# Attention and recurrence on TensorE in one written order instead of the scheduler's

## Chip, cores, metric

The kernel runs on one core of one Trainium2 chip. The metric is the device time of one execution in microseconds (us); less is better. TensorE multiplies and transposes, VectorE (DVE), ScalarE (ACT) and GpSimd (POOL) do the elementwise work, SyncE (SP) issues the DMAs.

## The reference

One decoder layer over 2048 tokens of 1024 channels, float32. `h = RMSNorm(x)` is projected once, and four groups of mixers read slices of the projection:

```python
# A, 4 heads of 64: stick-breaking attention, strictly causal
z = q @ k.T * scale;  between = reverse cumsum of log_sigmoid(-z), own term taken off
attn = where(strict, exp(log_sigmoid(z) + between), 0);  out = attn @ v
# B: chunked causal gating (128x128 mixing)
# C, 4 heads of 64: RWKV-7, over time t
sa = -state @ kk_t
state = state * d_t + sa (kk_t a_t)^T + v_t k_t^T;  y_t = state @ r_t
# D, 4 heads of 64: softmax attention with a cumulative log-forget bias, causal
probs = softmax(logits + cum_q - cum_k);  out = probs @ v
x = x + concat(A, B, C, D) @ W_out
x = x + HierMoE(RMSNorm(x));  return RMSNorm(x)
```

## The kernel before

The program has four stages in a row: `in_proj` (the projection), then attention (A and D) together with the recurrence (C), then `out_proj` (the product with W_out, the norm and the router), then the experts. The change is in the second stage, which in the profile lies between some 585 and 1528 us.

**Attention.** `attention` (a generator) walks over 8 heads, first the 4 stick-breaking heads (`sb`), then the 4 softmax heads. A head has 8 blocks `b` of 256 queries (two tiles of 128), and a block has `b // 2 + 1` chunks of up to 512 keys. This document calls the work for one block and one chunk a *step*; there are 20 for a head and 160 in all. A step consists of three pieces on TensorE:

- the *front*: logits of the two query tiles against the chunk, `logits`, lines 375 and 376 (keys are split in a high and a low part), with the mask added on the diagonal by line 378. Behind it, for a stick-breaking head, ScalarE takes a tanh (390), GpSimd an affine map (391) and VectorE a scan from the chunk's end backwards (393, `S`); for a softmax head VectorE adds the key bias and keeps the running maximum (402), and when a tile's last chunk is there, `softmax` forms the bias (408, 409), ScalarE the exponentials with their sums (413), VectorE the reciprocal (415, 416).
- the *transposes* of `S` (line 425), up to 4 per pair of key tiles, into a PSUM bank, which ScalarE copies to SBUF (`tq`, 427).
- the *value products* (line 431), which take `tq` and accumulate in the one bank `o`. When a block is complete, `out` adds its two halves and writes to DRAM (445, 456, 457).

In the old text transposes and value products of a pair stand together in `weigh`. Four PSUM banks serve logits and transposes, one `o`, three the recurrence; 12 SBUF tiles hold `S`.

**Recurrence.** `rwkv` computes C in 8 units (4 quarters of the sequence, 2 pairs of heads). A unit has two `group` generators (two chunks of 128 tokens each, the second one starts two rounds later), the `post` of the last unit and the `front` of the next. `interleave` advances all of them by one piece in turn; this document calls that a *round*, a unit has 24. In a group: two transposes and products (777 to 780), 24 score products (770, in three parts), five levels that invert a triangular matrix in small blocks (832 and 834, then 845; 849 and 850 in the last level), 864 and 870, then 877, 883, 892 to 896, and the state update `M` (913 to 917, 920). Between two levels VectorE works alone: 837 and 839 make `xe` and `yv`, which 845 needs; 846 and 847 make `xc`, which the next 832 needs. Unit 0 is written within `in_proj`.

**What sets the order.** In the program's text units 1 to 7 of the recurrence stand in one piece, then 60 steps of attention, then `route_setup` (tables in DRAM), then the other steps. The framework's scheduler sorts the instructions of every engine by its own estimate of when each can run; nothing is pinned.

```python
            for _ in rw:
                pass
            mix = attention(tc, K, left, sT, sV, cumD, mixT)
            for _ in range(60):
                next(mix)
            route_setup(tc, init, table, gtab, xacc)
            for _ in mix:
                pass
```

Of the kernel before, what the change touches and what calls it, by code (L numbers as in the profile page):

```python
# [307 lines left out]
def attention(tc, K, ctx, sT, sV, cumD, mixT):  # L308
# [17 lines left out]
    class Head:  # L326
# [54 lines left out]
        def spans(self, i):  # L381
            n = (i + 1) * 128
            return [(c, c * 512, min(512, n - c * 512)) for c in range(i // 4 + 1)]

        def sticks(self, i, c, S):
            x0 = c * 512
            w = min(512, (i + 1) * 128 - x0)
            z = self.logits(i, c, w)
# [7 lines left out]
        def softmax(self, i, S, rq):  # L396
            mx = None
            for c, x0, w in self.spans(i):
                z = self.logits(i, c, w)
                S[c] = sp.tile([128, 512], F32, name="S", tag="S")  # L400
                m = tp.tile([128, 1], F32, name="m")
                nc.vector.tensor_tensor_reduce(S[c][:, :w], z, self.nk[c][:, :w], 0.125,
                                               -3.0e38 if mx is None else mx, op0=OP.add, op1=OP.max, accum_out=m)
                mx = m
                yield
            c1 = cq[:, i, self.h:self.h + 1]
            bias = tp.tile([128, 1], F32, name="bias")
            nc.vector.tensor_add(bias, mx, c1)
            nc.vector.tensor_sub(bias, c1, bias)  # L409
            sm = tp.tile([128, 4], F32, name="sm")  # L410
            n = i // 4 + 1
            for c, x0, w in self.spans(i):
                nc.scalar.activation(S[c][:, :w], S[c][:, :w], AF.Exp, bias=bias, accum_out=sm[:, c:c + 1])  # L413
            if n > 1:
                nc.vector.tensor_reduce(sm[:, 0:1], sm[:, 0:n], AX.X, OP.add)
            nc.vector.reciprocal(rq, sm[:, 0:1])

        def weigh(self, b, p, S, o, first, last):
# [7 lines left out]
            tq = tp.tile([128, 512], F32, name="tq")  # L426
            nc.scalar.activation(tq[:, :w], t[:, :w], AF.Copy)  # L427
            for e in range(2):
# [32 lines left out]
        def block(self, b):  # L461
            S = [{}, {}]
            rq = None if self.sb else tp.tile([128, 2], F32, name="rq")
            o = []

            def weigh(p, first, last):
                if first:
                    o.append(po.tile([128, 256], F32, name="o"))
                self.weigh(b, p, S, o[0], first, last)
                if last:  # L470
                    self.out(b, o[0], rq)

            def front(c):
                if b % 2 == 0 and c == b // 2:
                    self.load(c)
                for a in range(2):
                    S[a][c] = sp.tile([128, 512], F32, name="S", tag="S")
                    self.sticks(2 * b + a, c, S[a])
                    yield

            def back(c):
                for p in range(min(2 * c + 1, b), 2 * c - 1, -1):
                    weigh(p, p == b, p == 0)
                    yield

            def front0():
                if b % 2 == 0:
                    self.load(b // 2)
                yield from self.softmax(2 * b, S[0], rq[:, 0:1])

            def mid():
                yield from self.softmax(2 * b + 1, S[1], rq[:, 1:2])

            def back0():
                for p in range(b + 1):
                    weigh(p, p == 0, p == b)
                    yield

            if self.sb:
                return [([front(c)], [], back(c)) for c in range(b // 2, -1, -1)]  # L500
            return [([front0()], [mid()], back0())]

    prev = iter(())
    for sb in (True, False):
        for h in range(NH):
            H = Head(h, sb)
            for b in range(8):
                for first, second, back in H.block(b):
                    for g in first:
                        yield from g  # L510
                    for g in second:
                        for _ in prev:
                            yield
                            next(prev, None)
                            next(g, None)
                        yield from g
                    yield from prev
                    prev = back
    yield from prev


CK = 128
# [83 lines left out]
def rwkv(tc, K, R, ctx, sT, prm, mixT):  # L606
# [358 lines left out]
    def interleave(*gens):  # L965
        gens = list(gens)
        while gens:
            for g in list(gens):
                try:
                    next(g)  # L970
                except StopIteration:
                    gens.remove(g)

    units = [(q, c) for q in range(4) for c in range(2)]
    sh, cur, last = [], [], None
    interleave(front(0, 0, sh, cur))
# [5 lines left out]
    for n, (q, c) in enumerate(units):  # L982
# [10 lines left out]
        interleave(*jobs)  # L993
        if n == 0:
            yield
        last, cur = (q, c, y, bon, sg), nxt
    interleave(post(*last))


# [806 lines left out]
def model(ctx, tc, x, xT, g1, w_in, wsT, bT, mu, w0, w2, a0, a2, g2, k_k, k_a, r_k, gn_w, gn_b, bf, w_out, g2b,  # L1806
# [15 lines left out]
    with tc.tile_pool(name="r_consts", bufs=1) as rp:  # L1822
# [71 lines left out]
```

## Time and profile before

| | us |
|---|---|
| median of 3 runs (lowest, highest) | 2600.77 (2600.74, 2604.18) |
| the profiled execution: its own time | 2600.24 |
| its span, first to last instruction | 2598.5 |
| TensorE busy / VectorE busy in the span | 2444.1 / 1679.6 |
[...]

The span is what the trace shows; 1.74 us lie around it. Busy time of TensorE is the union of its matmuls with modelled ends, so a busy TensorE may still be slowed by its clock or by gaps in its pipeline. A wait is put down to the instruction that came last.

### The profile page before, as it was taken

How to read it: one execution, taken by the hardware profiler on the slowest of the kernel's cores; microseconds unless marked ns; L12 is line 12 of the kernel's file. 1: busy time of each engine (PE TensorE's matmuls, PEld its weight loads, DVE VectorE, ACT ScalarE, POOL GpSimd, SP SyncE). 2: the span in 40 equal slices, each digit the busy share in tenths (PEclk: the TensorE clock that was granted, in tenths of full speed). 3: DMA queues.
4: the chain of work that ended last, by engine and by line, in shares of the span. 5: the costliest groups of instructions: out<-in, count | busy, mean ns of one | idle time of the engine just before them, and what ended most of it. 6: DMA issues, size and time to landing. Idle time of an engine off the chain costs nothing. (4 is left out here: it accounts for less than half of the span.)

```text
span 2598.5 us, 42227 instructions
## 1 busy us (share of the span) xinstructions
PE 2444.1 (94%) x14802; PEld 1753.0 (67%) x14803; DVE 1679.6 (65%) x3881; ACT 1322.4 (51%) x2527; POOL 677.1 (26%) x691
## 2 busy tenths in 40 slices
PE   8999999997989899999999999997999999999994
PEld 6789998874646464656556668874666676676663
DVE  5313402247797879786685756665777787787785
ACT  6201222224665564575566642222666776777774
POOL 2000000016364646331331022222212232222224
PEclk9999999998989998999999999998999999999997
DMA  8510222215121111111101056744979899899995
GB/s 258 163 63 26 80 69 67 71 60 124 35 53 29 47 39 39 47 50 47 49 27 48 10 171 180 234 139 114 339 263 352 309 320 368 292 324 356 328 316 169
DMA packets 241826, 394.73 MB, mean 152 GB/s; under 512 B 65921, under 2 KB 106753, under 8 KB 241608
## 3 DMA queue, kind: packets, MB, share of 16 engines
q1 hardware_dynamic: 222472, 336.68, 39.2%
q0 software_dynamic: 19136, 55.30, 7.6%
q8 instruction: 118, 1.93, 0.3%
q14 instruction: 100, 0.82, 0.1%
HBM read 319.24 MB, written 76.85 MB: 152 GB/s over the span
## 5 line engine op out<-in xcount | busy, mean ns | idle before, releaser
L72 DVE TENSOR_TENSOR wl<-wr,wh 128x1024 fp32r<-128x1024 f32 x366 | 442.4, 1222 | 116.9 <-ACT wh L71 106.8
L71 ACT ACTIVATE wh<-wr 128x1024 fp32r<-128x1024 f32 x366 | 381.4, 1057 | 150.7 <-PE pg L1456 57.9
L393 DVE TENSOR_TENSOR_SCAN S<-S,zero 128x512 f32<-128x512 f32 (+3 forms) x160 | 198.5, 1251 | 48.8 <-POOL S L391 48.6
L152 PE MATMUL p<-hhi,wh 128*128 128x512 f32 x512 | 205.5, 403 | 11.6 <-ACT hhi L112 6.5
L427 ACT ACTIVATE tq<-bk 128x512 f32<-128x512 f32 (+1 forms) x288 | 156.4, 571 | 103.6 <-PE bk L425 83.6
L425 PE MATMUL bk<-ident,S 128*128 128x128 f32 x1088 | 185.1, 291 | 25.0 <-DVE S L393 19.1
L153 PE MATMUL p<-hlo,wh 128*128 128x512 f32 x512 | 205.0, 400 | 0.0
L154 PE MATMUL p<-hhi,wl 128*128 128x512 f32 x512 | 204.5, 400 | 0.0
L431 PE MATMUL o<-tq,v 128*64 128x256 f32 (+1 forms) x1152 | 191.2, 403 | 4.5 <-ACT tq L427 2.6
L425 PEld LDWEIGHTS bk<-ident,S 128*128 128x128 f32 x1088 | 123.2, 144 | 100.7 <-issue 57.6
L156 DVE TENSOR_TENSOR e<-p,rb 128x512 f32<-128x512 f32 x64 | 43.6, 690 | 196.5 <-PE p L154 183.3
L391 POOL TENSOR_SCALAR S<-S 128x512 f32<-128x512 f32 (+3 forms) x160 | 125.6, 794 | 151.7 <-ACT S L390 136.5
L735 POOL TENSOR_TENSOR k<-big,k 128x512 f32<-128x512 f32 x8 | 14.2, 1772 | 550.6 <-DVE big L734 544.6
L375 PE MATMUL bk<-kh,qs 128*128 128x512 f32 (+2 forms) x320 | 148.1, 463 | 5.5 <-POOL qs L351 3.2
L171 PE MATMUL p<-wh,hhi 128*128 128x256 f32 (+1 forms) x512 | 144.5, 282 | 0.0
L172 PE MATMUL p<-wl,hhi 128*128 128x256 f32 (+1 forms) x512 | 144.4, 282 | 0.0
L173 PE MATMUL p<-wh,hlo 128*128 128x256 f32 (+1 forms) x512 | 143.7, 281 | 0.0
L152 PEld LDWEIGHTS p<-hhi,wh 128*128 128x128 f32 x512 | 97.6, 191 | 36.8 <-ACT hhi L112 6.2
L376 PE MATMUL bk<-kl,qs 128*128 128x512 f32 (+2 forms) x320 | 121.4, 381 | 0.0
L413 ACT ACTIVATE S<-S,bias 128x512 f32<-128x512 f32 (+3 forms) x160 | 103.6, 649 | 34.4 <-DVE bias L409 33.9
L71 ACT ACTIVATE wh<-raw 128x512 fp32r<-128x512 f32 (+1 forms) x52 | 27.7, 590 | 178.7 <-PE p L153 171.7
L1453 PE MATMUL pg<-wh,xh 128*128 128x512 f32 x248 | 102.6, 414 | 14.1 <-ACT s L1460 12.6
(559 smaller groups left out, 6153.5 us busy)
## 6 DMA issues: line engine op xcount, KB each, us to landing
wr<-in SPq DMA_DIRECT2D x386, 512.0 KB, 11.1
raw<-in SPq DMA_DIRECT2D x108, 256.0 KB, 4.1
sT<-e SPq DMA_DIRECT2D x64, 256.0 KB, 2.4
raw<-sT SPq DMA_DIRECT2D x128, 128.0 KB, 2.9
mr<-mixT SPq DMA_DIRECT2D x16, 512.0 KB
xt<-in SPq DMA_DIRECT2D x16, 512.0 KB
xacc<-xt SPq DMA_DIRECT2D x16, 512.0 KB, 4.8
h2D<-h SPq DMA_DIRECT2D x16, 512.0 KB, 8.6
```

Source lines behind the costliest of these rows:

```text
L71: nc.scalar.activation(hi, raw, AF.Copy)
L72: nc.vector.tensor_sub(lo, raw, hi.bitcast(F32))
L152: nc.tensor.matmul(p, wh[:, k, ms], hi[j][:, k], start=(k == 0), stop=False)
L153: nc.tensor.matmul(p, wh[:, k, ms], lo[j][:, k], start=False, stop=False)
L154: nc.tensor.matmul(p, wl[:, k, ms], hi[j][:, k], start=False, stop=(k == KD - 1))
L171: nc.tensor.matmul(p, a, wh[:, k], start=first and k == 0, stop=False, skip_group_check=True)
L172: nc.tensor.matmul(p, a, wl[:, k], start=False, stop=False, skip_group_check=True)
L375: nc.tensor.matmul(z[:, :w], q, self.kh[c][:, :w], start=True, stop=False)
L393: nc.vector.tensor_tensor_scan(r, r, K.zero.to_broadcast([128, w]), 1.0 if c == i // 4 else S[c + 1][:, 0:1], op0=OP.mult, op1=OP.add)
L425: nc.tensor.transpose(t[:, x:x + 128], S[a][j // 4][:, (j % 4) * 128:(j % 4) * 128 + 128], K.ident)
L427: nc.scalar.activation(tq[:, :w], t[:, :w], AF.Copy)
L431: nc.tensor.matmul(o[64 * e:64 * e + 64, o0:256], self.v[j // 4][:, j % 4], tq[:, x0:x1], start=first, stop=last, skip_group_check=True)
```

## The change

Units 1 to 7 of the recurrence now yield after every round, attention yields after every step, and both are written in turn under a block in which TensorE keeps the order of the text: 20 steps alone, `route_setup`, then 0.8 of a step per round until the recurrence is through (four rounds out of five are followed by one step, the fifth by none), then the rest. The other engines are still sorted by the scheduler.

Within attention a step is now written as front, value products of an earlier step, transposes of another: transposes come at least two steps (`LAG`) behind their front, value products one step behind their transposes. The two tiles' logits stand together. For a softmax head all chunks of a block get their fronts first, both tiles' bias, sum and reciprocal are made in one instruction each instead of two, and the transposes and products of the block follow one chunk per step. `tq`, `rq` and `m` have four buffers instead of three. The work on TensorE is the same, instruction by instruction.

```diff
-        def weigh(self, b, p, S, o, first, last):
+        def turn(self, b, p, S):
             t = bank()
...
-            tq = tp.tile([128, 512], F32, name="tq")
+            tq = tp.tile([128, 512], F32, name="tq", bufs=4)
             nc.scalar.activation(tq[:, :w], t[:, :w], AF.Copy)
+            return tq
+
+        def weigh(self, b, p, tq, o, first, last):
...
+    LAG = 2
+    ready, turned = [], []
+    n = 0
+
+    def step():
+        if turned:
+            t, weigh = turned.pop(0)
+            weigh(t)
+        if ready and ready[0][0] <= n - LAG:
+            turn, weigh = ready.pop(0)[1]
+            turned.append((turn(), weigh))
...
+                for front, backs in H.block(b):
+                    front()
+                    ready += [(n, f) for f in backs]
+                    step()
+                    n += 1
+                    yield
...
+ALONE = 20
+SHARE = 0.8
...
                 except StopIteration:
                     gens.remove(g)
+            yield
...
-            for _ in rw:
-                pass
             mix = attention(tc, K, left, sT, sV, cumD, mixT)
-            for _ in range(60):
-                next(mix)
-            route_setup(tc, init, table, gtab, xacc)
-            for _ in mix:
-                pass
+            with tc.manual_schedule(engines={mybir.EngineType.PE}):
+                for _ in range(ALONE):
+                    next(mix)
+                route_setup(tc, init, table, gtab, xacc)
+                due = 0.0
+                for _ in rw:
+                    due += SHARE
+                    while due >= 1.0:
+                        next(mix, None)
+                        due -= 1.0
+                for _ in mix:
+                    pass
```

Line numbers of the changed kernel: transposes 420, value products 430, and in the recurrence 11 more than before (832, 834, 845 are 843, 845, 856).

**First place: a stick-breaking head beside the levels of unit 1, on TensorE.** Before (375/376 logits, 425 transposes, 431 value products, 832/834 and 845 the two halves of a level; x4 means four times):

```order
L832 MATMUL bk<-ident,xc 128x128
L834 MATMUL bk<-bd_4722,xc 32x128 x4
L425 MATMUL bk<-ident,S 128x128 x2
L375 MATMUL bk<-kh,qs 128x512
L376 MATMUL bk<-kl,qs 128x512
L375 MATMUL bk<-kh,qs 128x512
L376 MATMUL bk<-kl,qs 128x512
L431 MATMUL o<-tq,v 64x256
L431 MATMUL o<-tq,v 64x128
L845 MATMUL bk<-xe,yv 32x128 x4
L425 MATMUL bk<-ident,S 128x128 x5
L845 MATMUL bk<-xe,yv 32x128 x4
```

The same unit now (420 transposes, 430 value products, 843/845 and 856 the halves of a level), one half of a level of both groups, a whole step, the next half:

```order
L856 MATMUL bk<-xe,yv 32x128 x8
L699 MATMUL bk<-ident,big 128x128 x4
L375 MATMUL bk<-kh,qs 128x512
L376 MATMUL bk<-kl,qs 128x512
L375 MATMUL bk<-kh,qs 128x512
L376 MATMUL bk<-kl,qs 128x512
L430 MATMUL o<-tq,v 64x256
L430 MATMUL o<-tq,v 64x128
L420 MATMUL bk<-ident,S 128x128 x8
L843 MATMUL bk<-ident,xc 128x128
L845 MATMUL bk<-bd_4708,xc 32x128 x4
```

Pieces of two, five and four rows became whole runs; from the first logits product to the last value product of the stage (transposes of `rq`, 455, apart as a kind of their own) runs of one kind number 1141 before and 669 now.

**Second place: a round without a step, in the same unit, now.** 843/845 of both groups and the 856 that needs their results through VectorE stand next to each other:

```order
L420 MATMUL bk<-ident,S 128x128 x8
L843 MATMUL bk<-ident,xc 128x128
L845 MATMUL bk<-bd_4708,xc 32x128 x4
L843 MATMUL bk<-ident,xc 128x128
L845 MATMUL bk<-bd_4722,xc 32x128 x4
L856 MATMUL bk<-xe,yv 32x128 x8
L375 MATMUL bk<-kh,qs 128x512
L376 MATMUL bk<-kl,qs 128x512
```

In the order before, attention lies between the two halves there, as the first fence shows.

**Third place: the end of a unit beside softmax heads.** Before, between the products 892 to 896 and the state update 913 to 917 of unit 5:

```order
L877 MATMUL bk<-kv,akT_4726 128x64 x4
L425 MATMUL bk<-ident,S 128x128 x6
L375 MATMUL bk<-kh,qs 128x256
L376 MATMUL bk<-kl,qs 128x256
L378 LDWEIGHTS identb
L378 MATMUL bk<-fx_mask,identb 128x128
L913 MATMUL bk<-qt,M_7793 64x128 x2
```

Now (888 for 877, 924 for 913):

```order
L888 MATMUL bk<-kv,akT_4726 128x64 x4
L375 MATMUL bk<-kh,qs 128x512
L376 MATMUL bk<-kl,qs 128x512
L375 MATMUL bk<-kh,qs 128x512
L376 MATMUL bk<-kl,qs 128x512
L430 MATMUL o<-tq,v 64x256 x4
L420 MATMUL bk<-ident,S 128x128 x7
L924 MATMUL bk<-qt,M_12786 64x128
```

More of attention now lies at the ends of the units. The table counts fronts (where the logits of one tile stand ahead of a mark and those of the other behind it, half a front). `A` is the stretch until unit 1 begins, `B` runs from the first 777 of a unit to the second group's 849, `C` from there to the next unit:

| stretch | before | now |
|---|---|---|
| A | 13 | 20 |
| B of units 1 to 3 | 55.5 | 36 |
| C of units 1 to 3 | 16.5 | 21 |
| B of units 4 to 7 | 64.5 | 48 |
| C of units 4 to 7 | 10.5 | 31 |
| behind the last unit | 0 | 4 |

## Rows read from the trace of the kernel before

**Rows 1.** The page's head and busy time: engine, us (share), instructions.

```profile
span 2598.5 us, 42227 instructions
PE 2444.1 (94%) x14802; PEld 1753.0 (67%) x14803; DVE 1679.6 (65%) x3881; ACT 1322.4 (51%) x2527; POOL 677.1 (26%) x691
```

**Rows 2.** B of units 1 to 3: busy PE, PEld, DVE, ACT, POOL; clock, DMA share, GB/s.

```profile
678.65:779.30 100.65, 87.68 (x620) 54.02 (x618) 92.13 (x160) 65.58 (x154) 54.60 (x55) 0.93 0.22 54
...
sum 302.35, PE 267.44 PEld 161.79 DVE 276.06 ACT 183.70 POOL 179.72; mean PE 89.14 PEld 53.93 DVE 92.02 ACT 61.23 POOL 59.91
```

**Rows 3.** The same view, C of units 1 to 3 (sum of three).

```profile
sum 105.20, PE 105.20 PEld 71.05 DVE 58.39 ACT 52.17 POOL 37.65; mean PE 35.07 PEld 23.68 DVE 19.46 ACT 17.39 POOL 12.55
```

**Rows 4.** The same view, B of units 4 to 7 (first of four, sum).

```profile
1086.20:1162.70 76.50, 73.08 (x556) 44.79 (x555) 66.50 (x223) 53.20 (x147) 25.06 (x24) 0.98 0.16 42
...
sum 300.30, PE 288.42 PEld 175.74 DVE 257.46 ACT 197.42 POOL 79.11; mean PE 72.10 PEld 43.93 DVE 64.37 ACT 49.36 POOL 19.78
```

**Rows 5.** The same view, C of units 4 to 7 (sum of four).

```profile
sum 125.80, PE 125.80 PEld 85.95 DVE 42.79 ACT 68.05 POOL 22.01; mean PE 31.45 PEld 21.49 DVE 10.70 ACT 17.01 POOL 5.50
```

**Rows 6.** The same view, stretch A and what follows the last unit.

```profile
585.00:678.65 93.65, 79.76 (x592) 50.51 (x592) 64.70 (x116) 44.17 (x105) 50.99 (x54) 0.89 0.41 90
1512.30:1530.00 17.70, 13.78 (x90) 8.13 (x90) 10.00 (x23) 11.81 (x18) 2.38 (x1) 0.92 0.63 213
```

**Rows 7.** Costliest groups, whole span: engine, shapes, count | busy, mean ns | idle before.

```profile
L393 DVE TENSOR_TENSOR_SCAN S<-S,zero 128x512 f32<-128x512 f32 (+3 forms) x160 | 198.5, 1251 | 48.8 <-POOL S L391 48.6
...
L425 PE MATMUL bk<-ident,S 128*128 128x128 f32 x1088 | 185.1, 291 | 25.0 <-DVE S L393 19.1
...
L431 PE MATMUL o<-tq,v 128*64 128x256 f32 (+1 forms) x1152 | 191.2, 403 | 4.5 <-ACT tq L427 2.6
```

**Rows 8.** Groups on VectorE, 580 to 1510 us.

```profile
L402 DVE CUSTOM_DVE_ANT_0 S<-bk,nk,m 128x512 f32<-128x512 f32 (+2 forms) x96 | 61.0, 635 | 25.6 <-PE bk L376 14.2 <-PE bk L378 10.8
...
L408 DVE TENSOR_TENSOR bias<-m,cq 128x1 f32<-128x1 f32 x64 | 18.2, 285 | 0.5
```

**Rows 9.** Timeline of TensorE at full clock: start, us, line, count.

```profile
702.34 0.50 PE L375 MATMUL bk<-kh,qs 128*128 128x512 f32 x1
702.68 0.39 PE L376 MATMUL bk<-kl,qs 128*128 128x512 f32 x1
702.91 0.39 PE L375 MATMUL bk<-kh,qs 128*128 128x512 f32 x1
...
703.37 1.02 PE L937 MATMUL bk<-sg,g 128*128 128x512 f32 x2
```

**Rows 10.** The same at 711.8 and 781.1 us.

```profile
711.78 1.08 PE L431 MATMUL o<-tq,v 128*64 128x256 f32 x8 [0.40 <-DVE oo L445]
712.79 0.38 PE L770 MATMUL bk<-ah,bh 64*128 64x256 f32 x1
...
781.11 1.03 PE L425 MATMUL bk<-ident,S 128*128 128x128 f32 x8
782.08 1.08 PE L431 MATMUL o<-tq,v 128*64 128x256 f32 x8
```

**Rows 11.** Timeline of TensorE in the levels of unit 1, waits in brackets.

```profile
737.63 0.43 PE L845 MATMUL bk<-xe,yv 128*32 128x128 f32 x8 [0.63 <-DVE yv L839]
739.16 0.77 PE L425 MATMUL bk<-ident,S 128*128 128x128 f32 x5 [1.10 <-DVE S L393]
741.14 0.43 PE L845 MATMUL bk<-xe,yv 128*32 128x128 f32 x8 [1.22 <-DVE yv L839]
```

**Rows 12.** Waits of TensorE, 580 to 1510 us: us in total, times, longest.

```profile
PE bk L425 <- DVE S L393: 19.1, 27, 2.6
PE bk L832 <- DVE xc L847: 10.7, 11, 4.7
PE bk L845 <- DVE yv L839: 10.1, 9, 2.7
```

**Rows 13.** Timeline of TensorE, the first product of the next stage.

```profile
1528.34 0.77 PE L1104 MATMUL p<-wh,mh 128*128 128x512 f32 x1 [0.23 <-DVE y L933]
```

More of the change, by code (lines that the diff above doesn't have):

```diff
@@ L379, in logits, with sticks @@
             return z[:, :w]
[L381 to L388, printed above, removed]
+        def sticks(self, i, c, z, S):
+            w = z.shape[-1]
             s = S[c][:, :w]
@@ L462, in block @@
             S = [{}, {}]
-            rq = None if self.sb else tp.tile([128, 2], F32, name="rq")
+            rq = None if self.sb else tp.tile([128, 2], F32, name="rq", bufs=4)
+            mx = [None]
             o = []
[L466 to L471, printed above, removed]
+            top = b // 2
@@ L473, in front @@
+            chunks = range(top, -1, -1) if self.sb else range(top + 1)
+            order = [[p for p in range(min(2 * c + 1, b), 2 * c - 1, -1)] for c in chunks]
+            ends = (order[0][0], order[-1][-1])
             def front(c):
-                if b % 2 == 0 and c == b // 2:
-                    self.load(c)
+                if b % 2 == 0 and c == chunks[0]:
+                    self.load(top)
+                z = []
                 for a in range(2):
+                    i = 2 * b + a
@@ L477, in front @@
                     S[a][c] = sp.tile([128, 512], F32, name="S", tag="S")
[L478 to L503, printed above, removed]
+                    z.append(self.logits(i, c, min(512, (i + 1) * 128 - c * 512)))
+                m = None if self.sb else tp.tile([128, 2], F32, name="m", bufs=4)
+                for a in range(2):
+                    if self.sb:
+                        self.sticks(2 * b + a, c, z[a], S[a])
+                    else:
+                        self.scores(c, z[a], S[a], None if mx[0] is None else mx[0][a], m[:, a:a + 1])
@@ new lines, in front, with turn, weigh @@
+                mx[0] = None if m is None else [m[:, a:a + 1] for a in range(2)]
+                if not self.sb and c == top:
+                    self.softmax(b, S, m, rq)
+            def turn(ps):
+                return [(p, self.turn(b, p, S)) for p in ps]
+            def weigh(t):
+                for p, tq in t:
+                    if p == ends[0]:
+                        o.append(po.tile([128, 256], F32, name="o"))
+                    self.weigh(b, p, tq, o[0], p == ends[0], p == ends[1])
+                    if p == ends[1]:
+                        self.out(b, o[0], rq)
@@ L504, in attention @@
+            backs = [(lambda ps=ps: turn(ps), weigh) for ps in order]
+            for k, c in enumerate(chunks):
+                yield (lambda: front(c)), ([backs[k]] if self.sb else backs if c == top else [])
+    LAG = 2
[8 more added lines that the diff above has]
+            turned.append((turn(), weigh))
     for sb in (True, False):
@@ L507, in attention @@
             for b in range(8):
[L508 to L519, printed above, removed]
+                for front, backs in H.block(b):
[4 more added lines that the diff above has]
+                    yield
+    while ready or turned:
+        step()
+        n += 1
+        yield
+ALONE = 20
+SHARE = 0.8
 CK = 128
@@ L972, in interleave, with run @@
                     gens.remove(g)
+            yield
+    def run(g):
+        for _ in g:
+            pass
     units = [(q, c) for q in range(4) for c in range(2)]
     sh, cur, last = [], [], None
-    interleave(front(0, 0, sh, cur))
+    run(interleave(front(0, 0, sh, cur)))
     yield
@@ L992, in rwkv @@
             jobs.append(front(*units[n + 1], sh, nxt))
-        interleave(*jobs)
         if n == 0:
+            run(interleave(*jobs))
             yield
+        else:
+            yield from interleave(*jobs)
         last, cur = (q, c, y, bon, sg), nxt
-    interleave(post(*last))
+    yield from interleave(post(*last))
 NE = 32
```

38 lines of the change are left out of this document (20 added, 18 removed).

## The prediction

> **What bounds the kernel now.** I read the page first: TensorE is busy 94% of the span, VectorE 65% [rows 1]. That is an average over stages, so I cut the stage of the change, 585 to 1528.34 us [rows 13], by the recurrence, with the view of busy time by stretch. A unit has two faces. In B (scores and levels) of the units that run beside stick-breaking heads, VectorE is busy 276.06 of 302.35 us, 91%, while TensorE has 35 us idle and a granted clock of 0.93 in the first of the three [rows 2]: VectorE sets the pace. In C (the unit's end) TensorE is busy in all of 105.20 us at full clock, VectorE in 58.39 [rows 3]: TensorE sets it. Beside softmax heads TensorE is the bound in both, 288.42 of 300.30 us in B [rows 4] and all of 125.80 us in C [rows 5], with VectorE at 86% in B. So the work that fills one engine alternates with work that fills the other, and a change of order can gain in two ways: by evening this out, and by making TensorE's own stream denser.
>
> The list of TensorE's waits is short: 19.1 us for scans, 10.7 and 10.1 us for the levels of the recurrence [rows 12]. In unit 1 they take 0.6 to 1.2 us each [rows 11].
>
> **The prices.** A step costs TensorE, from start to start at full clock: logits 703.37 - 702.34 = 1.03 us [rows 9], eight value products 712.79 - 711.78 = 1.01 us, eight transposes 782.08 - 781.11 = 0.97 us [rows 10]. A mean step has 1152/160 = 7.2 value products and 1088/160 = 6.8 transposes [rows 7], so 1.03 + 0.91 + 0.82 = 2.76; I take **2.8 us**. On VectorE a stick-breaking step costs two scans of 1.25 = **2.5 us** [rows 7], a softmax step at least two maxima of 0.635 = 1.3 us [rows 8].
>
> **The steps that move.** By the table of fronts in the section on the change:
>
> - A: 7 more steps on a TensorE that has nothing else to take up: 7 x 2.8 = +19.6.
> - B of units 1 to 3: 55.5 - 36 = 19.5 fewer. VectorE loses 19.5 x 2.5 = 48.8 us of 276.06; at its present share of 91.3% that is -53.4. TensorE would then have 267.44 - 54.6 = 213 us of work in 249, so VectorE stays the bound; TensorE's busy share hardly changes (86% for 88%), and I leave the clock as it was.
> - C of units 1 to 3: 4.5 more, TensorE bound: +12.6.
> - B of units 4 to 7: 16.5 fewer, TensorE bound: -46.2. VectorE falls by at least 16.5 x 1.3 = 21 to 236, of 254 us left; the batched bias takes half of line 408's 18.2 us more off it [rows 8]. It comes near to being the bound, so nothing more is credited.
> - C of units 4 to 7: 20.5 more: +57.4.
> - Behind the last unit: 4 more: +11.2.
>
> Together **+1.2 us**. The moves alone are worth nothing: a step that leaves VectorE's stretch saves 2.7 us there and costs 2.8 elsewhere. This is the main reason why I expect little from so large a change.
>
> **Runs of one kind.** The first product of a run takes longer: the first of the logits 702.68 - 702.34 = 0.34 us, the third, of the same shape, 0.23 [rows 9]. I take 0.1 us for a change of kind. The order has 1141 runs before and 669 now, 472 fewer, 47 us if TensorE were the bound everywhere. It is outside B of units 1 to 3, in 943 - 302 = 641 us or 68% of the stage; the runs taken as evenly spread, **-32 us**. Bounds: 0, if the slower start only moves to another place, and -47. I take the middle because the row shows the delay itself.
>
> [...]
>
> **Rounds without a step.** Seven units of 24 rounds, one in five without a step behind it: 34 places where a round stands directly behind the one whose results it needs (second fence of the change: 856 behind 843 and 845). There TensorE must wait for VectorE's `xe` and `yv` or `xc`. B is some 15 rounds long, so 9 of the 34 lie in B of units 1 to 3, where VectorE is the bound anyway and the wait is in its time already. For the other 25 the nearest rows are the waits of the same lines before, 10.1/9 and 10.7/11 or about 1.0 us [rows 12]: **+25 us**. Bounds: 0, since some rounds don't need the one ahead, and 25 x 2.7 = 68 by the longest wait of line 845, when scans stand ahead of `yv` in VectorE's queue. Behind the waiting product the logits of the next step stand, and so all of attention.
>
> **Waits that go.** Transposes come two steps behind their logits, so waits for the scan or the maximum vanish outside the VectorE-bound stretches. TensorE's idle time in B of units 4 to 7 is 300.30 - 288.42 = 11.9 us [rows 4]; I credit two thirds, **-8 us** (bounds 0 and -12). What is late next there is the recurrence's own chain, priced above.
>
> Costed at nothing: stretch A's slow start, 14 us of idle time at a clock of 0.89 [rows 6], is the tail of unit 0 and the first loads, and its order hardly changes. The last chunks run without the recurrence between them, each product waiting for ScalarE's copy; before, the end had 4 us of idle time too [rows 6]. The DMAs of the heads' loads stand where they stood relative to the steps. `route_setup` moves 40 steps forward, onto queues with room.
>
> **Sum.** 1.2 - 32 + 25 - 8 = -13.8 us on the profiled execution's 2600.24 us: **2586 us**. The median of the runs is 0.5 us higher than that execution, so the same number stands for it.
>
> **Rivals.**
>
> 1. *It evens out better than I credit.* In B of units 1 to 3 scans are now always two steps ahead of need, so VectorE might run at 98%: (276.06 - 48.8)/0.98 = 232 instead of 249, -17; no wait in rounds without a step, -25; the rest of the idle time in B of units 4 to 7, -4. That is 2540. For it: VectorE's idle time before scans is put down to GpSimd and the chain ahead of it, 48.6 us [rows 7]. Against it: levels of both groups, which wait on TensorE themselves, stand in the same queue. Chance 0.20.
> 2. *Nothing nets.* The terms cancel within 5 us: 2600. For it: each is as large as the sum. Chance 0.13.
> 3. *Slower, by the rounds without a step.* VectorE takes its instructions in their order; where two scans (2.5 us) stand ahead of `yv`, the wait is nearer to 2.7 than to 1.0 us. At 2.7: +42, 2628. It turns the sign from 1.0 + 13.8/25 = 1.6 us a place. For it: the scheduler before always laid attention between the halves of a level, and still 10 us were lost there [rows 12]. Against it: beside softmax heads VectorE has gaps. Chance 0.17.
> 4. *Slower, because a change of kind is free.* The weight loads run ahead, and the delay seen at a run's first product is work that merely shows there: the term of -32 is 0, and the time 2618. [...] Chance 0.10.
>
> That the change doesn't do what it says is excluded by the order of the instructions.
>
> **How the numbers follow.** About 0.2% (5 us) can be told from no change. The forecast, 2570 to 2595, has 0.40, so faster is 0.40 + 0.20 = 0.60, same 0.13, slower 0.17 + 0.10 = 0.27. The range reaches from rival 1's price to between rivals 3 and 4: **2540 to 2624**; its own range, if the forecast holds, is 2570 to 2595.
>
> **What would show it.** In the changed profile C of the last units should be TensorE bound and longer, some 45 us each; B of units 1 to 3 shorter than 90 us each with VectorE above 90%; the stage should end near 1515 us instead of 1528. Line 856 should wait for `yv` and 843 for `xc` more than 21 us in all, about 1 us each. If the stretches that are TensorE bound come out no shorter per step, the term of the runs was wrong; if VectorE falls below 85% in B of units 1 to 3 while TensorE waits there, the order holds both up, and the prediction is wrong on the slow side.

## The result and the profile after

The changed kernel takes 2711.8 us (median of 4 runs, 2709.26 to 2714.4) against 2600.76 (median of 4). The ratio on record is 1.0443, 95% interval 1.0417 to 1.0469; the two medians alone give 1.0427. It is some 4.4% slower; the forecast was 2586 us and its range ended at 2624.

The page's head, which answers to [rows 1]: TensorE's busy share falls from 94% to 91%, VectorE's from 65% to 62%, over a span longer by 110.5 us. The mean granted clock of TensorE falls from 0.968 to 0.939 (1 is the full clock).

```profile
span 2709.0 us, 42141 instructions
PE 2475.5 (91%) x14802; PEld 1801.8 (67%) x14803; DVE 1670.2 (62%) x3761; ACT 1323.8 (49%) x2527; POOL 655.6 (24%) x691
```

The first product of the output projection comes at 1629.92 us, before at 1528.34 [rows 13]: 101.6 of the 110.5 us were lost in the stage of the change. The other 8.9 us lie in the stages behind it and are not explained. The stage's stretches follow in the view of busy time by stretch (length, busy PE, PEld, DVE, ACT, POOL, clock, DMA): B of units 1 to 3 (third and sum), C of the same, B of units 4 to 7 (second and sum), C of the same, A, and what follows the last unit.

```profile
964.20:1053.54 89.34, 70.52 (x499) 45.67 (x497) 76.10 (x144) 46.21 (x116) 50.62 (x53) 0.85 0.20 52
sum 261.03, PE 211.87 PEld 135.91 DVE 221.78 ACT 142.55 POOL 129.20; mean PE 70.62 PEld 45.30 DVE 73.93 ACT 47.52 POOL 43.07
...
sum 127.17, PE 122.88 PEld 84.88 DVE 66.29 ACT 61.30 POOL 37.10; mean PE 40.96 PEld 28.29 DVE 22.10 ACT 20.43 POOL 12.37
...
1213.90:1298.28 84.38, 74.96 (x501) 48.06 (x499) 64.30 (x190) 48.02 (x134) 34.10 (x35) 0.80 0.22 60
...
sum 315.23, PE 269.48 PEld 175.42 DVE 234.64 ACT 178.22 POOL 111.82; mean PE 67.37 PEld 43.85 DVE 58.66 ACT 44.55 POOL 27.95
...
sum 166.87, PE 157.93 PEld 109.26 DVE 73.01 ACT 81.19 POOL 5.97; mean PE 39.48 PEld 27.31 DVE 18.25 ACT 20.30 POOL 1.49
...
585.00:704.40 119.40, 101.02 (x730) 65.34 (x730) 86.00 (x134) 60.88 (x139) 65.00 (x71) 0.90 0.33 77
1574.70:1629.90 55.20, 42.98 (x256) 26.51 (x254) 20.50 (x71) 31.67 (x77) 2.93 (x34) 0.88 0.33 95
```

| stretch | before | forecast by the moves alone | after |
|---|---|---|---|
| A | 93.65 | 113.3 | 119.4 |
| B of units 1 to 3 | 302.35 | 249.0 | 261.0 |
| C of units 1 to 3 | 105.20 | 117.8 | 127.2 |
| B of units 4 to 7 | 300.30 | 254.1 | 315.2 |
| C of units 4 to 7 | 125.80 | 183.2 | 166.9 |
| behind the last unit | 16.0 | 27.2 | 55.2 |

B of units 4 to 7 holds 16.5 fewer fronts and is longer all the same. TensorE is idle there for 315.23 - 269.48 = 45.8 us (before 11.9 [rows 4]), at a clock of 0.80 to 0.88 (before 0.93 to 1.00).

The same view of the whole stage, cut at the last unit's end, gives the balance. After:

```profile
585.00:1574.80 989.80, 863.29 (x6251) 570.91 (x6251) 681.73 (x1568) 524.24 (x1333) 349.09 (x375) 0.89 0.16 43
...
sum 1044.90, PE 906.17 PEld 597.32 DVE 702.22 ACT 555.81 POOL 352.02; mean PE 453.09 PEld 298.66 DVE 351.11 ACT 277.90 POOL 176.01
```

Before:

```profile
585.00:1514.90 929.90, 868.83 (x6423) 546.48 (x6424) 700.22 (x1733) 547.40 (x1395) 369.49 (x379) 0.95 0.18 46
...
sum 943.30, PE 878.72 PEld 552.01 DVE 707.70 ACT 555.84 POOL 370.17; mean PE 439.36 PEld 276.00 DVE 353.85 ACT 277.92 POOL 185.08
```

TensorE's idle time rose from 943.30 - 878.72 = 64.6 to 138.7 us, its busy time by 27.5. Part of the busy time ran at a lower clock, 0.50, and took longer for it: from 850.15 us, at 0.50, the products of line 781 start 0.21 us apart; before, as line 770, at a clock of 1.00, they start 0.12 us apart from 701.66 us. A first estimate of that loss is width times (1 - clock), summed over windows of 5 us: 44 us before and 118 after; the table of the experiments uses it. It also counts time at the lower clock in which TensorE was idle. Half of the busy time at 0.50 alone is 41 us before and 105 after, and by this second estimate the same work at full clock would take 837 us before and 801 after. So the denser stream **saved** some 37 us, idle time cost 74 and the clock 64: +101. Both estimates take work at half clock to last twice as long; the products of line 781 took 1.8 times as long, so both are probably too high.

What TensorE waits for in the stage (us in total, times, longest), to be held against [rows 12]:

```profile
PE o L430 <- ACT tq L422: 28.4, 20, 5.4
PE bk L843 <- DVE xc L858: 15.8, 10, 4.7
PE bk L856 <- DVE yv L850: 13.4, 13, 3.0
PE bk L790 <- DVE rkT L815: 11.2, 5, 6.8
PE o L430 <- DVE oo L444: 9.7, 6, 2.1
PE bk L699 <- DVE big L695: 8.0, 3, 5.3
```

Gone are the 19.1 us for scans. New are waits of value products for ScalarE's copies `tq` and of the recurrence for a bank (790 needs one that line 815 reads last) and for the small-number chain of its rsqrt (699). The timeline of TensorE shows what such a wait holds up (start, us, operation, wait in brackets):

```profile
1009.95 0.66 PE L856 MATMUL bk<-xe,yv 128*32 128x128 f32 x16
1015.87 1.08 PE L699 MATMUL bk<-ident,big 128*128 128x128 f32 x4 [5.26 <-DVE big L695]
1016.74 0.42 PE L843 MATMUL bk<-ident,xc 128*128 128x128 f32 x1
...
1018.67 0.69 PE L375 MATMUL bk<-kh,qs 128*128 128x384 f32 x1
...
1605.59 1.09 PE L420 MATMUL bk<-ident,S 128*128 128x128 f32 x8
1612.04 1.97 PE L430 MATMUL o<-tq,v 128*64 128x256 f32 x8 [5.36 <-ACT tq L422]
```

At 1015.87 four transposes of one piece stand 5.26 us, with the next half levels of both groups and a step's logits behind them. At 1612.04 the products stand right behind their transposes, and ScalarE's timeline shows why `tq` is late: eight exponentials of the next block, 1605.86 to 1611.4, stand ahead of it.

```profile
1605.86 0.72 ACT L405 ACTIVATE S<-S,bias 128x512 f32<-128x512 f32 x1 [1.48 <-DVE bias L399]
...
1610.70 0.70 ACT L405 ACTIVATE S<-S,bias 128x512 f32<-128x512 f32 x1
...
1611.41 1.05 ACT L422 ACTIVATE tq<-bk 128x512 f32<-128x512 f32 x2
```

### The profile page after: what moved, and what is told of

The parts are those of the page before. It is cut to its first block, busy times and chain, and to the rows that moved or that the text cites. A ratio compares the mean times of both kernels' runs of the same rounds, so it can differ in the third digit from the quotient of the medians.

```text
span 2709.0 us, 42141 instructions
## 1 busy us (share of the span) xinstructions
PE 2475.5 (91%) x14802; PEld 1801.8 (67%) x14803; DVE 1670.2 (62%) x3761; ACT 1323.8 (49%) x2527; POOL 655.6 (24%) x691
## 5 line engine op out<-in xcount | busy, mean ns | idle before, releaser
L430 PE MATMUL o<-tq,v 128*64 128x256 f32 (+1 forms) x1152 | 184.6, 426 | 44.1 <-ACT tq L422 28.4
L420 PEld LDWEIGHTS bk<-ident,S 128*128 128x128 f32 x1088 | 130.8, 152 | 61.2 <-issue 44.3
L420 PE MATMUL bk<-ident,S 128*128 128x128 f32 x1088 | 169.3, 299 | 2.2 <-DVE S L387 1.5
L385 POOL TENSOR_SCALAR S<-S 128x512 f32<-128x512 f32 (+3 forms) x160 | 113.0, 716 | 193.5 <-ACT S L384 182.1
L430 PEld LDWEIGHTS o<-tq,v 128*64 128x64 f32 x1152 | 77.3, 150 | 113.1 <-ACT tq L422 41.6
L376 PE MATMUL bk<-kl,qs 128*128 128x512 f32 (+2 forms) x320 | 128.6, 402 | 0.0
```

Source lines behind the costliest of these rows:

```text
L420: nc.tensor.transpose(t[:, x:x + 128], S[a][j // 4][:, (j % 4) * 128:(j % 4) * 128 + 128], K.ident)
L430: nc.tensor.matmul(o[64 * e:64 * e + 64, o0:256], self.v[j // 4][:, j % 4], tq[:, x0:x1], start=first, stop=last, skip_group_check=True)
```

## The experiments

Each run is compared with the kernel before on its own chip (medians there 2591 to 2594 us), so ratios are compared, not medians; a hundredth is 26 us. "Idle" and "clock" are TensorE's idle time and the first estimate of the clock's cost, in us, in the stage up to the last multiple of 5 us.

| run | edit | median, us | ratio, 95% interval | idle | clock |
|---|---|---|---|---|---|
| before | | | 1 | 63 | 44 |
| after | | 2711.8 | 1.0443 [1.0417, 1.0469] | 137 | 118 |
| e1_free | nothing pinned | 2607.2 | 1.0059 [1.0037, 1.0082] | 76 | 48 |
| e3_steps_only | nothing pinned, text order of before | 2600.7 | 1.0023 [1.0007, 1.0038] | 68 | 61 |
| e2_att_pinned | attention alone pinned | 2606.1 | 1.0057 [1.0036, 1.0077] | 91 | 58 |
| e5_rec_pinned | recurrence alone pinned | 2625.6 | 1.0131 [1.0113, 1.0149] | 84 | 75 |
| e4_each_round | share 0.94, no steps ahead | 2696.7 | 1.0385 [1.0341, 1.0429] | 130 | 126 |
| e6_exp_spread | exponentials by chunk | 2682.4 | 1.0354 [1.0322, 1.0386] | 128 | 106 |
| e7_thirds | finer weave | 2661.1 | 1.0284 [1.0252, 1.0316] | 129 | 90 |
| e8_bank_moved | a bank to the scores | 2702.9 | 1.0423 [1.0405, 1.0441] | 140 | 113 |
| e17_only_two_behind | products two steps behind | 2675.0 | 1.0320 [1.0294, 1.0346] | 125 | 94 |
| e10_thirds_spread | e7 and e6 | 2662.1 | 1.0272 [1.0222, 1.0321] | 119 | 89 |
| e12_thirds_spread_late | e10, 699 a round later | 2646.8 | 1.0195 [1.0155, 1.0234] | 117 | 89 |
| e13_share | e12, share 0.9 | 2645.0 | 1.0204 [1.0184, 1.0225] | 118 | 94 |
| e14_two_behind | e12, products two steps behind | 2599.1 | 1.0026 [1.0011, 1.0040] | 89 | 67 |
| e16_fill | idle time filled | 2717.2 | 1.0490 [1.0465, 1.0515] | 115 | 87 |
| e9_att_pinned_spread | e2 and e6 | 2585.3 | 0.9972 [0.9949, 0.9995] | 83 | 38 |
| e11_free_spread | e3 and e6 | 2610.3 | 1.0061 [1.0036, 1.0087] | 78 | 63 |
| e15_two_o | e9, two banks for `o` | 2619.9 | 1.0107 [1.0090, 1.0124] | 88 | 56 |
| e18_att_two_behind | e9, products two steps behind | 2615.1 | 1.0083 [1.0063, 1.0103] | 75 | 81 |

**Is it the fixed order?** Three runs undo it in parts.

```diff
-            with tc.manual_schedule(engines={mybir.EngineType.PE}):
+            if True:
```

> The changed program with TensorE's order left to the scheduler; the text, the new steps of attention and ScalarE's order of work within a step stay. Theory P (the fixed order makes TensorE stand before a late recurrence product while attention work behind it is ready, and the idle pieces drop its clock): about 1,040 runs of one kind again, TensorE's idle time in the stage falls from about 139 us towards the 65 us of the kernel before, the first product of the output projection comes below 1570 us and the time is between 2600 and 2650 us. Rival S (the new step form is to blame: a block's eight exponentials stand ahead of the copies tq on ScalarE): the waits of line 430 for tq stay above 25 us and the time stays above 2680 us.

1.0059, 1,039 runs of one kind (pieces of only logits, only transposes, only value products or only recurrence), the first product at 1534.4 us, idle time 76, the waits for `tq` 3.8 us: theory P on every point. The order pinned on TensorE costs 3.8 hundredths, 100 us. Without the guard the scheduler also sorts the other engines differently, so this is the price of the pinned order with what the scheduler makes of the others under it; no run separates the two.

```diff
+            for _ in rw:
+                pass
             mix = attention(tc, K, left, sT, sV, cumD, mixT)
-            with tc.manual_schedule(engines={mybir.EngineType.PE}):
...
+            for _ in range(60):
+                next(mix)
+            route_setup(tc, init, table, gtab, xacc)
+            for _ in mix:
+                pass
```

> Only the new step form of attention: all of the recurrence ahead in the text as in the kernel before, 60 steps, route_setup, and nothing pinned. It prices the step form by itself. Theory P: 2595 to 2625 us, so that the form costs 0 to 25 us and the order the rest of the 111 us. Rival S: 2670 us or more. The first product of the output projection would stand near 1530 us by P and near 1600 us by S.

1.0023, first product at 1532.0: the new steps by themselves cost next to nothing, and rival S falls as the cause of the whole. `e2_att_pinned` has this text with the guard around attention alone:

> The recurrence stands ahead of all of attention in the text and is left to the scheduler; attention's steps alone stand in a fixed order among themselves. Some 908 runs of one kind, between the 1,067 of the kernel before and the 595 of the changed one. Theory P (what costs is that recurrence products stand in TensorE's fixed order): the waits of lines 843, 856, 790 and 699 shrink below half of their 50 us in sum, the time is 2590 to 2640 us. Rival S (the step form): the waits for tq stay, above 2680 us. Rival W (any fixed order costs, because no order settled beforehand can follow what is late): above 2660 us with the waits now in attention's lines.

(The text's 1,067 and 595 are another count; by that of the section on the change it is 909 between 1141 and 669.) 1.0057. P's time holds, and W falls with it, but P's reason does not hold: lines 843, 856, 790 and 699 still wait 44 us in sum, for whatever releaser, against 60 in the changed kernel, 843 alone 23.6 us for `xc`. So a list of waits does not tell what an order costs. The mirror pins the recurrence, ahead of attention:

```diff
+            with tc.manual_schedule(engines={mybir.EngineType.PE}):
+                for _ in rw:
+                    pass
```

> The mirror of the run with attention's steps pinned: the recurrence's rounds, all ahead of attention in the text, stand in their fixed order among themselves (pieces of the two groups, of post and of front in turn), and attention's products go where the scheduler puts them. Theory I (the order within the recurrence is what costs: one late piece holds the ready pieces of the other generators): 2660 us or more. Theory C (the coupling costs: a fixed share of a step behind each round, whatever the round takes): 2600 to 2630 us, with TensorE idle for less than 95 us of the stage against 139 in the changed kernel, and the first product of the output projection before 1550 us.

1.0131, idle 84, the first product at 1558.7 us and not ahead of 1550: nearer to C. That is 1.1 hundredths above `e3_steps_only`, 28 us, but it does not price the recurrence's inner order: attention's last value product comes at 1489.6 us here, and from 1500 to 1555 us the recurrence is alone at a clock of 0.50, which by the estimate of the last section can have cost up to 27 us. With either stream pinned alone the kernel is slower by 1.3% or less; the other 81 us of the changed kernel appear only when **both** are tied to each other.

**What in the tie?** Edits of the changed kernel, everything pinned.

```diff
-            for c in range(n):
-                for a in range(2):
+            def exps(c):
+                for a in range(2):
...
+        if ready and not seen[0] and ready[0][0] <= n + 1 - LAG:
+            ready[0][1][2]()
```

> The changed kernel with one edit: a block's exponentials are no longer issued all at once behind its last scores, but those of one chunk at a time, one step ahead of the transposes that read that chunk. TensorE's order is the same. Theory E (the row of up to eight exponentials ahead of the copies tq on ScalarE makes the 28 to 32 us of waits of line 430 for tq): those waits fall below 12 us, the tail behind the recurrence's last product, 55 us in the changed kernel, falls below 35 us, and the time to 2665 to 2695 us. Theory C (the weave is what costs, ScalarE's order only shows it): the waits for tq become waits for something else, and the time stays within 12 us of 2712.

0.9 hundredths, 23 us: the time that E named, but the waits for `tq` fall only to 13.7 and the tail to 48.9 us, less than E asked. `e7_thirds` yields after each part of a step and each piece of a round:

```diff
-                for _ in rw:
-                    due += SHARE
+                for w in rw:
+                    due += 3 * SHARE * (w or 1)
```

> The same mean share, but a finer weave: a step is issued in three parts (logits, value products, transposes), and the parts stand between the single pieces of a round instead of whole steps between whole rounds. 847 runs of one kind in place of 670. Theory C in the form that the grain costs (a late piece has only the next piece of its own round behind it): TensorE's idle time in the stage falls from 139 us below 105, and the time to 2630 to 2680 us in spite of the added runs. Rival: the fixed order costs by itself whatever its grain, because no share fits every round: within 15 us of 2712, or slower by the 177 added runs, up to 18 us.

1.6 hundredths, 41 us, though with idle time 129 and not below 105: what fell is the clock's share, 118 to 90. Both together:

> Both edits together in the full fixed order: steps in thirds between the pieces of a round, and the exponentials spread. Alone they gave 51 and 29 us by the medians. If they are two costs that add up, 2625 to 2640 us, near the 1.0131 of the run in which the recurrence alone was pinned. If both only relieved the same waits, 2650 us or more. The waits for tq, 31.6 us with thirds alone, fall below 15.

1.0272: they do not add up; the waits for `tq` are still 22.8 us. What had not been touched is that value products stand one step behind their transposes, with a copy by ScalarE between. One line moves them to two, with a fifth buffer for `tq`:

```diff
-        if turned:
+        if len(turned) > 1 or turned and not ready:
...
-            tq = tp.tile([128, 512], F32, name="tq", bufs=4)
+            tq = tp.tile([128, 512], F32, name="tq", bufs=5)
```

> The changed kernel with one edit: value products two steps behind their transposes instead of one. Theory D (the distance is a cost by itself, 48 us in the run with the three other edits): 2650 to 2675 us, the waits for tq below 10 us and the tail behind the recurrence shorter than the 55 us of the changed kernel by 10 us or more. Rival (it needs the finer weave and the spread exponentials): within 12 us of 2712.

Alone 1.2 hundredths, 32 us; the waits for `tq` fall to 3.9 us, the tail only to 49, six less. Theory D at its weak end, and short of its sign for the tail. First `e12_thirds_spread_late` gives the rsqrt's transposes one `yield` more of distance:

> As the run with thirds and spread, and one round more of distance ahead of the four transposes of the recurrence's rsqrt (line 699 of the changed kernel), which wait 8 us (17.9 us with thirds) for VectorE's chain of small operations. Theory I (what the fixed order of the recurrence still costs are pieces that stand too near to what they wait for): those waits fall below 5 us and the time 8 to 25 us below that of the run with thirds and spread. Rival: post and front come a round later and hold up the next unit: no gain.

0.8 hundredths, 20 us (the intervals of the two ratios overlap a little); line 699's waits fell from 18.2 to 12.3 us, not below 5. On top of it, the two steps:

> The same run (2647 us), with the value products two steps behind their transposes instead of one. Theory D (distance: in a fixed order a product costs what it stands too near to its operand): the 23 us of waits for tq fall below 8 and the time by 10 to 25 us, to 2622 to 2637. Rival: ScalarE's queue delivers tq late whatever the distance, or the longer tail takes it back: within 8 us of 2647.

1.0026: 44 us more, beyond what D asked. The stage of this run:

```profile
585.00:1489.60 904.60, 818.10 (x6251) 552.53 (x6251) 676.49 (x1573) 523.32 (x1341) 357.74 (x375) 0.93 0.18 47
1489.60:1529.40 39.80, 36.67 (x250) 24.24 (x250) 19.29 (x67) 27.85 (x66) 2.93 (x34) 0.96 0.38 120
```

and its waits:

```profile
PE bk L863 <- DVE xc L878: 20.6, 11, 3.4
PE bk L810 <- DVE rkT L835: 13.9, 5, 5.3
PE bk L876 <- DVE yv L870: 10.3, 9, 2.7
```

A fully pinned order thus comes within 0.3% of the kernel before, though it keeps both streams tied. The recurrence still waits as it did (863, 810 and 876 are 843, 790 and 856 here), but attention's products no longer do, and idle time is 89 instead of 137 us. The parts do not add up: 41 and 23 alone, 44 together, 32 alone and 44 on top.

**Other suspects.**

> Same fixed order, but no 20 steps of attention ahead of the recurrence and a share of 0.94 in place of 0.8, so that nearly every round is followed by a step. Rival R (what costs are the 25 rounds that no step follows, priced at 1.0 us each and at most 68 us): 25 to 70 us faster than the changed kernel, 2640 to 2690 us. Theory P: little to gain, within 25 us of the changed kernel's 2712 us, since the recurrence products still stand ahead of whatever is ready; stretch A alone shrinks.

15 us, below what R asked. But this run has a loss of its own, shown in the last section: the recurrence begins almost alone, at half clock for 95 us. So R's price is not measured here.

> The changed kernel with one bank of PSUM moved from attention (four to three) to the recurrence's scores (the second score tile of each head half gets a bank of its own from unit 1 on). Theory B (in a fixed order the scores stand until VectorE's masked copies of the tile before free a bank: 25 to 30 us of waits of lines 781, 790, 716 and 720 for rkT, rbT and kv): those waits fall below 10 us and the time by 10 to 40 us, with the clock's share, to 2670 to 2700 us. Rival: attention with three banks waits in their place (lines 375 and 420), no gain or up to 30 us slower.

1.0423, no measurable gain: 781 and 790 wait less, but line 699 waits for a bank instead (`rbT`, 9.9 us, `btok`, 6.2). The rival's result, though not by lines 375 and 420.

> The run with thirds, spread and the later transposes (2647 us, 1.0195), with a share of 0.9 of a step per round in place of 0.8, so that attention ends about with the recurrence. Theory T (the tail costs: 50 us of attention alone behind the recurrence's last product against 14 in the kernel before): the tail falls below 25 us and the time to 2620 to 2635 us. Rival: the added steps lengthen the units by as much, since TensorE and VectorE are both held up there: within 8 us of 2647.

The rival: the tail falls from 49.9 to 13.7 us, and the stage ends at 1573.8 instead of 1575.6. A tail is not a loss by itself.

```diff
+    def fill():
+        for j in range(3):
+            nc.tensor.transpose(spare[:, j * 128:j * 128 + 128], K.ident, K.ident)
...
                 for _ in rw:
+                    K.fill()
```

> The changed kernel with three transposes of the identity into a bank of their own behind every round, which nobody reads (attention then has three banks): some 165 x 3 x 0.27 us = 134 us of added work on TensorE, part of it in the 139 us in which it was idle. Theory K (the clock is a cost of its own: 117 us of the stage are lost to half clock, because TensorE was idle before): the loss falls below 80 us and the time stays within 2680 to 2740 us in spite of the added work. Rival (the clock only follows; what counts is when the pieces become ready, so that the filler delays them further): 2760 us or more.

516 useless transposes. The 134 us of the text are too much, since transposes overlap: eight take 0.97 us from start to start [rows 10], so 516 take some 62. The time rose by 0.5 hundredths, 12 us; the clock's loss fell from 118 to 87 (by the second estimate from 105 to 76), idle time from 137 to 115. About 50 of 62 us of added work were free. K missed its number of 80 and held its time. That the clock is a cost of its own is made likely, no more: attention also lost a bank here.

**A version below both.** `e9_att_pinned_spread` pins attention alone and spreads the exponentials.

> Only attention's steps in a fixed order among themselves (1.0057 of the kernel before), and the exponentials spread over the steps. If the row of exponentials is a cost of its own, its 11 us of waits for tq there fall below 5 us and the time comes to 2585 to 2600 us, at or below the kernel before; if the scheduler had already worked around it, no change from 1.0057, within 4 us.

0.9972 [0.9949, 0.9995], 7 us faster than the kernel before. Three relatives went the other way:

> Nothing pinned, the new steps of attention, the text in the order of before, and the exponentials spread: the candidate to beat the kernel before. The same steps without the spread stand at 1.0023. If ScalarE's row of exponentials costs there too, 2580 to 2590 us against 2591; if the scheduler hides it, 1.002 again.

> Only attention's steps pinned, exponentials spread (2585 us, 0.9972 of before), and one of attention's four banks moved to the value products, whose single bank o makes them wait 14 us for VectorE's read of the block before. If that wait is on the path: 2568 to 2580 us. If the three banks left for logits and transposes make TensorE wait in their place: 2585 to 2600.

> Only attention's steps pinned and exponentials spread (2585 us, 0.9972), with the value products two steps behind. The waits for tq were only 5 us there: by theory D no more than 5 to 10 us to gain, 2575 to 2585 us. Rival: the order of steps there is loose enough, and one more value product in flight only lengthens the end: 2585 to 2595.

1.0061, 1.0107 and 1.0083, each outside what was expected on either side. Where the scheduler sorts even one of the two, each edit sorts everything anew, and such a run cannot price the edit, nor can `e9_att_pinned_spread` itself; for two of the three the last section shows where time went. `e15_two_o` is not explained; there line 430's products (435) wait for `tq` 12.6 us instead of 5.2.

## Why the prediction was wrong

**Right in size, not in its price: the runs of one kind.** By the second estimate the stage's work at full clock fell from 837 to 801 us with 472 runs fewer; I had -32, bound -47. But 0.1 us for a change of kind does not come out of the runs: counted the same way, `e7_thirds` needs 792 us with 847 runs, less than the changed kernel with 669, and `e2_att_pinned` 802 us with 909. So it is in part luck that -32 came near, and what made the stream denser is open. Rival 4 falls by its term of 0; its mechanism is not decided. In the trace of the kernel before the weight load of line 937 begins at 703.14 us, 0.23 us ahead of its product, and that of line 375 at 702.34 us, together with its product; no run shows what a load ahead is worth at a change of kind.

**Wrong: "25 rounds without a step x 1.0" as the only wait that the fixed order adds.** I priced two lines. For `yv` and `xc` they wait 13.4 + 15.8 = 29.2 us against 20.8 before, so 8 us more and not 25, while TensorE's idle time rose by 74. The loss came from lines that I had costed at nothing or not named:

- "each product waiting for ScalarE's copy", excused by the end's 4 us of idle time. In the old text transposes and products stood in one routine too, but the scheduler laid other work between them. Pinned one step apart, they wait 28.4 us for `tq`. The distance alone is worth 32 us (`e17_only_two_behind`), and in the finer weave 44.
- The tie itself. I took TensorE's order as a count of steps per stretch, while a pinned order also says who stands behind whom: a late piece holds everything ready behind it, as at 1015.87 us. Left to the scheduler, the same steps cost 0.2 to 0.6%; tied, 4.4%. This is shown, and so is a part of it, the 32 to 44 us of the distance to `tq`.
- "I leave the clock as it was". The clock's cost grew from 41 to 105 us, by 64, nearly as much as the idle time. The bounds had no term for it.

**Wrong, but without effect on the sum: a front taken for a whole step.** In C of units 4 to 7 the trace has 18 fronts more up to the last product of line 924, but only 36 value products (five steps' worth) and 20 transposes (three) more: by my prices 25.5 us and not 57.4. TensorE's work at full clock rose by 27 us there, so 166.9 us instead of the 183.2 of the moves shows no denser stream. From B of units 4 to 7 there went 17.5 fronts, but only 48 value products and 40 transposes, 29 us and not 46.2; what I credited too much there I charged too much in C. With single pieces as they moved, the moves still add up to about +1 us.

The forecast failed most in B of units 4 to 7: -46.2 forecast, +14.9 measured. By these estimates the pieces account for -29, idle time for +34, the clock for +31 (10 before, 41 after), and the rest, -21, for the denser stream. In B of units 1 to 3 VectorE is busy 221.78 of 261.03 us, 85.0%, with TensorE idle 49 us: at the edge of the sign that I had named for an order that holds both up. Rival 3 had the right sign and the wrong place. I saw that all of attention stands behind a waiting product, and still gave the wait to one pair of lines, though every other late line stands in the same order.

What stays open: which pairs in the tie cost how much, since the edits do not add up, how much of the clock's 64 us would stay if no wait did, and what made the stream denser.

## To carry to other kernels

Before an order is written out by hand, list for each instruction what it waits for on another engine and how many microseconds of other work stand between; here one step of distance was too little for a copy on an engine with other work queued, and two took its waits from 28 us to 4. Price a fixed order by its late pieces and what stands behind them, and look at the granted clock besides, not only at the sum of its work. When one of two interleaved streams runs out, look at the clock of the other, alone.

## What the runs showed of the hardware that was not expected

Where the recurrence is alone on TensorE, or nearly so, the granted clock can stay at 0.50 for 45 to 95 us at a stretch, although the engine is busy for 78 to 87% of the time. In `e1_free` attention's last value product is at 1469.2 us, and TensorE is busy in 4.09 of the 6 us from 1469 to 1475. From there the clock is down, though TensorE, by the ends in the trace, is busy for 31 us of the 50 without a gap:

```profile
1475.00:1525.00 50.00, 40.15 (x241) 28.14 (x242) 15.80 (x46) 12.06 (x32) 0.00 (x0) 0.50 0.15 45
```

In `e18_att_two_behind`, attention's last product at 1476.6:

```profile
1480.00:1540.00 60.00, 50.79 (x323) 32.10 (x315) 23.68 (x64) 13.32 (x33) 0.00 (x0) 0.50 0.16 49
```

In `e5_rec_pinned`, attention's last product at 1489.6:

```profile
1500.00:1555.00 55.00, 45.26 (x287) 29.14 (x283) 19.29 (x56) 12.91 (x32) 0.00 (x0) 0.50 0.14 44
```

At the start of `e4_each_round`, with eight logits products of line 375 as the first of attention, and 0.43 us of work in the 5 us ahead of it:

```profile
605.00:700.00 95.00, 82.90 (x424) 55.41 (x425) 46.40 (x108) 34.00 (x88) 27.09 (x31) 0.50 0.34 70
```

In `e9_att_pinned_spread` attention lasts to 1499.9, and the same end of the last unit runs at full clock:

```profile
1450.00:1500.00 50.00, 48.39 (x422) 33.41 (x422) 21.50 (x70) 33.35 (x86) 0.38 (x4) 1.00 0.09 26
```

Being alone is not enough for it. In `e13_share` attention's last value product is at 1540.6, and the recurrence goes on alone at full clock, with TensorE busy in 17.59 of 19 us; the clock falls only behind that, where two waits of 3.0 and 7.0 us follow:

```profile
1541.00:1560.00 19.00, 17.59 (x150) 12.77 (x150) 4.38 (x12) 3.60 (x10) 0.00 (x0) 1.00 0.11 32
```

What lifts or keeps the clock is thus not settled by these rows.

By an estimate that takes work at 0.50 to last twice as long, the clock cost at most half of such a stretch: 25 us in `e1_free`, 27 in `e5_rec_pinned`, 30 in `e18_att_two_behind`, where the difference to `e9_att_pinned_spread` is 1.1 hundredths, 29 us. The sixteen products `bk<-rbT,wz` in it take 6.4 us in `e1_free` and 3.8 at full clock in `e9_att_pinned_spread`, less than twice as long. `e11_free_spread` has such a stretch too, from 1485 to 1530. So what sets these versions apart from `e9_att_pinned_spread` may be no more than that attention reaches to the end there. Why that one lies below the kernel before, whose attention reaches to the end as well, stays open.
